# Hybrid attention block on one core: order of the opening products, and one gating weight's subtraction moved to VectorE

## The chip, the cores and the metric

The kernel runs on one core of a Trainium2 chip. A core has a TensorE (PE, matrix products; PEld in the profile is its loading of weights), a VectorE (DVE), a ScalarE (ACT), a GpSimd (POOL) and a SyncE (SP), which here issues the DMA transfers. Each engine works through its own instruction queue in order and waits on semaphores for the others. The metric is the device time of one execution in microseconds (us): 604.07 for the kernel before, the median of three runs (603.5 to 606.83).

## The reference

One decoder layer on 512 tokens and 16 leading meta tokens, width 1024, in float32:

```
u    = RMSNorm(h)                      # h: meta tokens, then x
proj = u @ w_in                        # 7600 columns, split into the parts below
(cq, ckv, k_pe, z_mla, fq, fk, fv, f, z_fox, gate_a, gate_b) = split(proj)
q, k, v of MLA   from RMSNorm(cq) @ w_uq and RMSNorm(ckv) @ w_ukv, with rope on 32 dims
o_mla = causal_attention(q, k, v);      y_mla = (o_mla * silu(z_mla)) @ w_br_mla
o_fox = causal_attention(fq, fk, fv, + cumulative log forget gate from f)
y_fox = (o_fox * silu(z_fox)) @ w_br_fox
mixed = (sigmoid(gate_a) * y_mla + sigmoid(gate_b) * y_fox) @ w_out
h + RMSNorm(mixed), meta tokens dropped
```

Both branches have 16 heads.

## The kernel before

Every float32 operand of a product is split into an upper half (rounded to the format that TensorE takes) and a lower half (the rest), and each product is three products: upper by upper, lower by upper, upper by lower. The upper half of a weight (`wh`) is a cast on ScalarE (line 130), its lower half (`wl`) a subtraction, `split_lo` (line 103), on the engine that `low[0]` holds: GpSimd until the merge at the end, VectorE there. A unit of work (`unit`) has a `prep`, which does cast and subtraction of its weight, and a list of steps with TensorE's products; who calls `prep` early decides where the subtraction comes in the queues.

The opening turns five token tiles (0 to 3 with 128 tokens, 4 with the 16 meta tokens) into normalized, transposed features, `uTh` (upper, by ScalarE, line 382) and `uTl` (lower, by VectorE, line 379). Then `small` multiplies a tile's features by the narrow part of `w_in` (432 columns: latent query and key, rope key, forget gate). That weight comes in four chunks `wsr` of two row blocks each. Its upper half is `wsh`: chunks 0 to 2 are cast by GpSimd, chunk 3 by ScalarE after tile 1's features (`small_hi`, line 313). Its lower half is `wsl`: chunk 0 by GpSimd, chunks 1 to 3 by VectorE (`small_lo`, line 317). The products of tile t gather in the PSUM tile `psm` t; argument 2 of `small` says which of the three products are issued, argument 3 which of the eight row blocks. After them come `back` (the square sums at line 418, the rope pieces `tm` at line 423, which wait for the square sums, and the scalings) and `latent` (transposes).

The order on TensorE is the order in which the program is written (`manual_schedule`). The calls with `pin` also keep the written order on their engines; the other work on ScalarE, VectorE, GpSimd and SyncE is ordered by a scheduler that plans with estimated durations.

Then come 16 attention stages, FoX and MLA in turn for eight pairs of heads. A stage has the scores of its own pair (`st`), the softmax in two parts (`n0`, `n1`: exponentials, `ri`, the normalized weights `pn` as an upper half from ScalarE and a lower half from VectorE at line 823, and small pieces for the meta tokens, `mt`, on GpSimd), the transposes of `pn` into `pt` by DMA, and the product with the values (`ov`), which is issued in the next stage. Between them TensorE gets "fill": products that project the next pair (`mq`, `mk`, `fq`, `fk`, `v`) and the gating products (`z`). In the first stage (`si == 0`) the preparation of the next two weights of the fill, `mq`'s and that of the second gating product, is called between `n0()` and `n1()`. After the stages the merge multiplies by the branch weights and `w_out`.

Of the kernel before, what the change touches and what calls it, by code (L numbers as in the profile page):

```python
# [27 lines left out]
KD = D // 128  # L28
# [26 lines left out]
def block_kernel(ctx: ExitStack, tc: tile.TileContext, x, meta_tokens, pre_norm_g, w_in, fox_forget_b,  # L55
                 mla_q_norm_g, mla_kv_norm_g, w_uq, w_ukv, w_br_mla, w_br_fox, w_out, post_norm_g,
                 rope_tok, rope_pe, out):
    nc = tc.nc
# [37 lines left out]
    def mm(*a, **k):  # L96
        nc.tensor.matmul(*a, **k)  # L97
# [25 lines left out]
    low = [nc.gpsimd]  # L123
# [46 lines left out]
    def acc(name):  # L170
        return accp.tile([128, 512], F32, tag="acc", name=name)
# [49 lines left out]
    def run(steps):  # L221
        for _, fn in steps:
            fn()
# [48 lines left out]
    with ExitStack() as ph:  # L272
# [124 lines left out]
        def small(t, which, ks=range(KD)):  # L397

            d0, q0 = (META + 128 * t, 0) if t < 4 else (0, R_Q)
            if t not in psms:  # L400
                psms[t] = acc("psm4")[:, 0:NSM] if t == 4 else pps.tile([128, NSM], F32, tag="psm", name=f"psm{t}")
            ts = slice(d0, d0 + 128)
            for k in ks:
                for q, (u, w) in enumerate(((uTh, wsh), (uTl, wsh), (uTh, wsl))):
                    if q in which:
                        mm(psms[t][:, q0:], u[:, k, ts], w[:, k, q0:], start=(k == 0 and q == 0),
                           stop=(k == KD - 1 and q == 2))
# [68 lines left out]
        turned(1, 1, range(KD), pin)  # L476
        pin(small_hi(3, nc.scalar.copy))
        small(0, (1,), range(2))
        small(0, (0, 1), range(2, KD))
        small(1, (0, 1))  # L480
        for c in (1, 2, 3):
            pin(small_lo(c, nc.vector))
        squares(2, pin)
# [72 lines left out]
    with ExitStack() as att:  # L556
# [352 lines left out]
        for si, (br, pr) in enumerate(stages):  # L909
            s0, s1, n0, n1, va = attention(br, pr)  # L910

            fill = fills[si]
            for fn in [s0] + late:
                fn()
            if si == 0:
                run(fill[:3])
            s1()

            if si == 0:

                run(fill[3:5])
                run(vts[1, 0] + pe_rest)
                n0()
                for ahead_ in [fn.prep for _, fn in fill[5:] if hasattr(fn, "prep")][:2]:
                    ahead_()
                n1()
                first_t.extend(through)
                run(fill[5:])
            else:
                if si == 1:  # L930

                    written[0] = True
                    for x in range(2):
                        store0(x, 2, 8)
                    written[0] = False
                run(fill[:5])
                if si == 1:

                    behind[:] = exps[:1]
                if si == 2:  # L940
                    behind.clear()
                n0()
                run(fill[5:11])
                if br:

                    behind[:] = [halved[("k", 1, pr), 1]]
                run(fill[11:12])
                if br:
                    behind.clear()
                n1()  # L950
                if 6 <= si < 8:

                    written[0] = True
                    rest1(si - 6)
                    written[0] = False
                run(fill[12:])
            written[0] = False
            if si == 1:

                behind[:] = [halved[("k", 1, 1), 0]]  # L960
            late = [va]
# [232 lines left out]
```

## Time and profile before

| | |
|---|---|
| median of three runs | 604.07 us (603.5 to 606.83) |
| profiled execution | 606.64 us, of which the span is 604.9 us |
| PE busy | 592.8 us (98%) |
| DVE, ACT, POOL busy | 375.2, 342.9, 180.8 us (62%, 57%, 30%) |
| opening | until the first scores at 59.84 us |
| first attention stage | 59.84 to 81.31 us |
| moved by DMA | 93.25 MB |

The span is the time from the first to the last instruction of the profiled execution; its own time is 1.74 us longer. A busy share is a sum over the instructions of an engine. An entry such as "PE z <- POOL wl" in the list of waits says that TensorE stood idle before a product that writes `z` until GpSimd had finished `wl`; its numbers are the total, the count and the longest. Where a line of the timeline carries brackets, they hold the idle time before it and what ended it.

### The profile page before, as it was taken

To read this page: it belongs to the slowest core of one execution; us is meant where nothing else is said; L and a number is where in the kernel's file an instruction comes from. 1 tells how busy PE (TensorE), PEld (TensorE's weight loads), DVE (VectorE), ACT (ScalarE), POOL (GpSimd) and SP (SyncE) were. 2 spreads that over 40 slices of the span, in tenths; PEclk is the share of its full clock that TensorE was granted. 3 is DMA by queue.
4 is the path that set the end of the run, shared out by engine and by line. 5 is a ranking of instruction groups with operands and counts; after the bars stand their busy time and mean duration, and the time that the engine had idled before them with its cause. 6 is when DMAs were issued, how large, how long until landed. Compare 5 with 4: busy or idle time off the path is not lost.

```text
span 604.9 us, 11000 instructions
## 1 busy us (share of the span) xinstructions
PE 592.8 (98%) x3777; PEld 503.7 (83%) x3777; DVE 375.2 (62%) x1003; ACT 342.9 (57%) x786; POOL 180.8 (30%) x240
## 2 busy tenths in 40 slices
PE   8999999999999999999999999999999999999996
PEld 6989789889889888788898898887888888888884
DVE  6846776774775775755756657773833624367857
ACT  7846775784674775755766748761221433243653
POOL 4316644444348453523433534530000000000000
PEclk9999999999999999989999999999999999999999
DMA  8533589789796898988797885987633323322603
GB/s 295 113 79 106 123 198 215 182 198 205 108 191 163 162 180 186 165 194 165 132 177 170 168 184 136 198 169 258 194 105 104 101 77 101 104 98 91 232 0 140
DMA packets 219960, 93.25 MB, mean 154 GB/s; under 512 B 133420, under 2 KB 211636, under 8 KB 219904
## 3 DMA queue, kind: packets, MB, share of 16 engines
q1 hardware_dynamic: 219904, 92.55, 66.3%
q8 instruction: 30, 0.49, 0.3%
q14 instruction: 26, 0.21, 0.1%
HBM read 58.10 MB, written 4.00 MB: 103 GB/s over the span
## 4 chain that ended last, share of the span: by engine, by line
PE 95%; DVE 2%; ACT 1%; POOL 1%; DMA 1%; issue 0%; DVEq 0%; POOLq 0%; ACTq 0%
PE z L97 15%; PE py L97 14%; PE pg L97 14%; PE v L97 9%; PE st L97 8%; PE fk L97 8%; PE fq L97 7%; PE ov L97 5%; PE x L97 4%; PE psm L97 3%; PE mq L97 2%; PE mk L97 1%; PE ppe L97 1%; PE spun L97 1%; PE y L97 1%; PE pt L100 1%
## 5 line engine op out<-in xcount | busy, mean ns | idle before, releaser
L103 POOL TENSOR_TENSOR wl<-wraw,wh 128x1024 fp32r<-128x1024 f32 (+2 forms) x63 | 122.6, 1954 | 106.2 <-ACT wh L130 74.4
L130 ACT CAST wh<-wraw 128x1024 fp32r<-128x1024 f32 (+1 forms) x80 | 83.1, 1041 | 116.7 <-PE pg L97 38.5
L823 DVE SCALAR_TENSOR_TENSOR pn<-sf,ri,pn 128x128 f16<-128x128 f32 (+3 forms) x128 | 70.8, 593 | 13.8 <-ACT pn L822 13.7
L795 ACT ACTIVATE sf<-sf,nb 128x144 f32<-128x144 f32 (+3 forms) x128 | 72.0, 564 | 11.1 <-DVE nb L787 10.9
L822 ACT ACTIVATE pn<-sf,ri 128x128 f16<-128x128 f32 (+3 forms) x128 | 61.5, 551 | 20.1 <-ACT sf L795 17.3
L103 DVE TENSOR_TENSOR wl<-wraw,wh 128x1024 fp32r<-128x1024 f32 x33 | 40.3, 1222 | 41.2 <-ACT wh L130 41.1
L787 DVE CUSTOM_DVE_ANT_0 sf<-st,maskt 128x272 f32<-128x272 f32 (+2 forms) x128 | 48.7, 435 | 4.2 <-PE st L97 4.1
L97 PE MATMUL z<-uTh,wl 128*128 128x512 f32 x128 | 50.1, 391 | 1.1 <-POOL wl L103 1.1
L97 PE MATMUL z<-uTh,wh 128*128 128x512 f32 x128 | 50.9, 398 | 0.0
L97 PE MATMUL pg<-uTh,wh 128*128 128x512 f32 x128 | 50.3, 393 | 0.0
L97 PE MATMUL z<-uTl,wh 128*128 128x512 f32 x128 | 50.0, 391 | 0.0
L97 PE MATMUL pg<-uTl,wh 128*128 128x512 f32 x128 | 49.8, 389 | 0.0
L97 PE MATMUL pg<-uTh,wl 128*128 128x512 f32 x128 | 49.8, 389 | 0.0
L97 PE MATMUL py<-gh,wh 128*128 128x512 f32 x128 | 49.8, 389 | 0.0
L97 PE MATMUL py<-gl,wh 128*128 128x512 f32 x128 | 49.8, 389 | 0.0
L97 PE MATMUL py<-gh,wl 128*128 128x512 f32 x128 | 49.8, 389 | 0.0
L97 PE MATMUL st<-hlk,hlq 64*128 64x272 f32 (+3 forms) x480 | 48.0, 310 | 0.0
L97 PEld LDWEIGHTS st<-hlk,hlq 64*128 64x128 f32 x480 | 35.7, 189 | 5.9 <-ACT vh L719 2.8
L700 DVE TENSOR_REDUCE vsc<-v 128x1 f32<-128x272 f32 (+1 forms) x32 | 13.2, 432 | 37.9 <-PE v L97 37.9
L97 PE MATMUL v<-uTh,wl 128*128 128x256 f32 (+1 forms) x128 | 36.5, 285 | 0.0
L97 PE MATMUL fk<-uTl,wh 128*128 128x256 f32 (+1 forms) x128 | 36.5, 285 | 0.0
L97 PE MATMUL fk<-uTh,wh 128*128 128x256 f32 (+1 forms) x128 | 36.4, 285 | 0.0
(233 smaller groups left out, 1432.4 us busy)
## 6 DMA issues: line engine op xcount, KB each, us to landing
wraw<-in_w_in_dram SPq DMA_DIRECT2D x56, 512.0 KB, 4.4
wraw<-in_w_br_fox_dram SPq DMA_DIRECT2D x8, 512.0 KB, 3.5
tb<-in_w_out_dram SPq DMA_DIRECT2D x8, 512.0 KB, 8.2
wraw<-in_w_br_mla_dram SPq DMA_DIRECT2D x8, 512.0 KB, 3.5
wraw<-in_w_out_dram SPq DMA_DIRECT2D x6, 512.0 KB
pt<-pn SPq DMA_TRANSPOSE x128, 3.2
xr<-in_x_dram SPq DMA_DIRECT2D x4, 512.0 KB, 6.0
out_dram<-yo SPq DMA_DIRECT2D x8, 256.0 KB, 2.0
```

The lines of the kernel that those rows point to most:

```text
L97: nc.tensor.matmul(*a, **k)
L100: nc.tensor.transpose(*a)
L103: return eng.tensor_tensor(out=lo, in0=src, in1=f32(hi), op=ALU.subtract)
L130: nc.scalar.copy(wh[:, :n], raw[:, :n])
L700: nc.vector.tensor_reduce(out=sc[:, i : i + 1], in_=ps, op=ALU.max, axis=AX.X, apply_absolute_value=True)
L787: nc.vector.tensor_tensor_reduce(out=sf_of(h, b)[:, c0 : c0 + w], in0=ps[h][:, o : o + w], in1=maskt[:, m0 : m0 + w], scale=-scale, scalar ...
L795: exps[g] = nc.scalar.activation(sf, sf, AF.Exp, bias=sums["nb"][:, h, b : b + 1], scale=-1.0, accum_out=sums["su"][:, h, b : b + 1]).ins
L822: nc.scalar.activation(hi, sf, AF.Copy, scale=rib)
L823: nc.vector.scalar_tensor_tensor(out=lo, in0=sf, scalar=rib, in1=hi, op0=ALU.mult, op1=ALU.subtract)
```

## The change

Two edits. In the opening, the products of the features' upper and lower halves with `wsh` (products 0 and 1) were issued for all of tile 0 and then for all of tile 1; now both tiles' row blocks up to 5, which use chunks 0 to 2, come first, and the row blocks 6 and 7 of both tiles, which use chunk 3, after them. In the first attention stage, `low[0]` is VectorE while the two preparations between `n0()` and `n1()` are called. `mq`'s preparation names GpSimd itself and is not touched; the second gating weight's lower half is now subtracted on VectorE.

```diff
         small(0, (1,), range(2))
-        small(0, (0, 1), range(2, KD))
-        small(1, (0, 1))
+        small(0, (0, 1), range(2, 6))
+        small(1, (0, 1), range(6))
+        small(0, (0, 1), range(6, KD))
+        small(1, (0, 1), range(6, KD))
         for c in (1, 2, 3):
             pin(small_lo(c, nc.vector))
...
                 n0()
+                low[0] = nc.vector
                 for ahead_ in [fn.prep for _, fn in fill[5:] if hasattr(fn, "prep")][:2]:
                     ahead_()
+                low[0] = nc.gpsimd
                 n1()
```

On TensorE 12 products of tile 1 (`psm1`) now stand ahead of the last four of tile 0 (`psm0`); the number of products is the same. The scheduler also orders ScalarE differently in the opening. In the piece below, of ScalarE's queue, `psm` is tile 0's, `hn_301` is the normalization of token tile 3, `sm_315` and `st_0_316` take tile 0's square sums, and line 332 is the square root behind each sum.

```order
 L332 ACTIVATE st_4_296<-st_4_296,eps_t 16x1
+L418 ACTIVATE sm_315,st_0_316<-psm_216 128x256
 L352 ACTIVATE hn_301,st_3_302<-ht_148 128x1024
-L418 ACTIVATE sm_315,st_0_316<-psm_216 128x256
+L418 ACTIVATE sm_315,st_0_316<-psm_216 128x128
 L332 ACTIVATE st_3_302<-st_3_302,eps_t 128x1
-L418 ACTIVATE sm_315,st_0_316<-psm_216 128x128
-L382 ACTIVATE uTh<-pt_0_330,gcol 128x128
 L332 ACTIVATE st_0_316<-st_0_316,eps_t 128x2
```

Tile 3's square sum stands now between the two square sums of tile 0's features, where it stood ahead of both, and its square root moves back with it. On VectorE the scaling of `hn_301` moves back in the same way, to stand between the `tm` pieces.

In the first attention stage VectorE's queue held, before, after the second part's `ri_872`: the two lower halves `pn_725`, the finishing of the first gate `sil_1049`, the lower halves of the next query and key.

```order
L803 TENSOR_SCALAR su_871<-su_871 128x2
L804 RECIPROCAL ri_872<-su_871 128x2
L823 SCALAR_TENSOR_TENSOR pn_725<-sf_923,ri_872,pn_725 128x4x128 x2
L736 SCALAR_TENSOR_TENSOR sil_1049<-sil_1049,z_961 128x512
L103 TENSOR_TENSOR hlq_1061<-mq_1054,hlq_1061 128x512
L103 TENSOR_TENSOR hlk_1080<-mk_1076,hlk_1080 128x272
```

The same place of VectorE's queue now (`wl_1012` is the second gating weight's lower half):

```order
L805 TENSOR_SCALAR su_871<-su_871 128x2
L806 RECIPROCAL ri_872<-su_871 128x2
L103 TENSOR_TENSOR wl_1012<-wraw_855,wh_1011 128x1024
L825 SCALAR_TENSOR_TENSOR pn_725<-sf_923,ri_872,pn_725 128x4x128
L738 SCALAR_TENSOR_TENSOR sil_1049<-sil_1049,z_961 128x512
L825 SCALAR_TENSOR_TENSOR pn_725<-sf_923,ri_872,pn_725 128x4x128
L103 TENSOR_TENSOR hlq_1061<-mq_1054,hlq_1061 128x512
L103 TENSOR_TENSOR hlk_1080<-mk_1076,hlk_1080 128x272
```

The subtraction stands ahead of both `pn_725`, and `sil_1049` has come between them. On GpSimd `wl_1012` is gone from its place behind the small pieces of `pn_725`. On SyncE a load of a later weight no longer waits for GpSimd, and in the next stage the transpose of `vh` into `vp` goes ahead of a load of `CT`. From the third stage on the queues are the same.

## The prediction

> **What bounds the kernel now.** I read the page first (busy shares), then the waits of TensorE over the whole span, then the timeline of each engine round the places where TensorE waits.
>
> ```profile
> span 604.9 us, 11000 instructions
> PE 592.8 (98%) x3777; PEld 503.7 (83%) x3777; DVE 375.2 (62%) x1003; ACT 342.9 (57%) x786; POOL 180.8 (30%) x240
> ...
> PE spun L97 <- DVE ONE L236: 2.1, 1, 2.1
> PE ov L97 <- issue: 1.2, 1, 1.2
> PE ov L97 <- DMA pt<-pn: 1.2, 1, 1.2
> PE z L97 <- POOL wl L103: 1.1, 1, 1.1
> PE psm L97 <- ACT wsh L313: 0.6, 1, 0.6
> ```
>
> TensorE is busy 98% of the span, and the list of its waits is short: 2.1 us at the very start, 2.4 us before one product of attention weights and values (`ov`), 1.1 us before a gating product (`z`) and 0.6 us before a feature product of the opening (`psm`). The change speaks to the last two. No other engine can give more than what such waits hold, since TensorE keeps its instruction count.
>
> The time is worked out against the profiled execution, 606.64 us (span 604.9 and 1.74 around it). That is 2.57 us above the median of 604.07, nearly the 2.4 us of the `ov` wait. I take it that the ordinary run lacks most of that wait; one profile cannot prove it. Differences found in this execution are put on the median.
>
> **Part 1, the opening.** In these timeline rows the columns are start, duration, engine, line and operation.
>
> ```profile
> 11.80 0.36 PE L97 MATMUL psm<-wsh,uTh 128*128 128x432 f32 x1
> 12.00 0.36 PE L97 MATMUL psm<-wsh,uTl 128*128 128x432 f32 x1
> 13.01 0.46 PE L97 MATMUL psm<-wsh,uTh 128*128 128x432 f32 x1 [0.65 <-ACT wsh L313]
> ...
> 7.79 4.36 ACT L382 ACTIVATE uTh<-pt,gcol 128x128 fp32r<-128x128 f32 x16
> 11.99 0.96 ACT L313 CAST wsh<-wsr 128x864 fp32r<-128x864 f32 x1
> ...
> 9.15 4.21 DVE L379 SCALAR_TENSOR_TENSOR uTl<-pt,gcol,uTh 128x128 fp32r<-128x128 f32 x16
> 13.29 2.98 DVE L317 TENSOR_TENSOR wsl<-wsr,wsh 128x864 fp32r<-128x864 f32 x3
> ```
>
> These products follow each other every 0.20 us (11.80 to 12.00). After the one at 12.00 the next could start at 12.20; it started at 13.01, since it reads the fourth chunk's upper half, which ScalarE finished at 11.99 + 0.96 = 12.95. So the hole costs 13.01 - 12.20 = 0.81 us.
>
> The change puts 12 products of token tile 1 there, 12 x 0.20 = 2.4 us, from 12.20 to 14.6, when the fourth chunk has been ready for 1.6 us. They need tile 1's features. Their upper halves are the last eight of ScalarE's 16, done by 12.15. Their lower halves are the last eight of VectorE's 16 at 4.21 / 16 = 0.263 us: chunk 0 at 9.15 + 9 x 0.263 = 11.52 (needed at 12.40), chunk 5 at 12.83 (needed at 14.4). The cover is full, so 0.81 us comes forward. The work queued behind (VectorE's three lower halves of the small weights, 13.29 to 16.27) waits for the fourth chunk, not for TensorE, and does not move; the last is due at 14.6 + 8 x 0.20 + 6 x 0.20 = 17.4.
>
> What is late next is tile 4's lower features. The scheduler now puts the square sum of `hn3` on ScalarE behind the first square sum of the features, and VectorE's pieces follow.
>
> ```profile
> 17.17 1.06 ACT L352 ACTIVATE hn<-ht 128x1024 f32<-128x1024 f32 x1 [1.29 <-DVE hn L358]
> 18.83 0.38 ACT L418 ACTIVATE sm<-psm 128x256 f32<-128x256 f32 x1 [0.51 <-PE psm L97]
> 19.54 0.20 ACT L418 ACTIVATION_READ_ACCUMULATOR sm<-psm 128x1 f32 x1
> ...
> 20.44 0.75 DVE L358 TENSOR_SCALAR hn<-ht,st 128x1024 f32<-128x1024 f32 x1
> 21.10 0.41 DVE L423 TENSOR_TENSOR tm<-psm,rt 128x16 f32<-128x16 f32 x4
> 21.50 0.21 DVE L103 TENSOR_TENSOR uTl<-um,uTh 128x64 fp32r<-128x64 f32 x1
> ...
> 21.88 0.24 PE L97 MATMUL psm<-wsh,uTh 128*128 128x176 f32 x1
> 21.96 0.28 PE L97 MATMUL psm<-wsh,uTl 128*128 128x176 f32 x1
> ...
> 24.96 1.04 PE L100 MATMUL pt<-ident,hn 128*128 128x128 f32 x8
> ```
>
> Tile 0's features end 0.81 earlier, so the first square sum starts at 18.02, not 18.83. Then `hn3` takes ScalarE for about 1.06 us, the second square sum reads out by about 19.8, and VectorE's `tm` pieces, which wait for it, start there. The `hn3` scaling (its neighbours show 0.66 us from its start to the next start) falls between them, so the lower half `uTl<-um` comes at 19.8 + 0.2 (two `tm`) + 0.2 (reciprocal) + 0.66 + 0.2 (last `tm`, reciprocal) = 21.05 and ends at 21.26. TensorE, 0.81 us earlier, wants it for the product of 21.96 at 21.05 with its load before. So about 0.2 us is given back; bounds are 0 (the old order would have it at 20.9) and the whole 0.81. I take 0.2, which the rows of these very instructions give. **Part 1: 0.81 - 0.2 = 0.6 us.** Later pieces of the opening (transposes of tile 3 need `hn3`, which is done at about 21.0 and was used at 24.96) move forward with TensorE, which by the list of its waits has none from there to the `z` product of part 2.
>
> **Part 2, the first attention stage.**
>
> ```profile
> 72.83 0.40 PE L97 MATMUL z<-uTh,wh 128*128 128x512 f32 x1
> 73.07 0.39 PE L97 MATMUL z<-uTl,wh 128*128 128x512 f32 x1
> 74.57 0.50 PE L97 MATMUL z<-uTh,wl 128*128 128x512 f32 x1 [1.11 <-POOL wl L103]
> 76.67 0.28 PE L97 MATMUL mk<-cTh,wh 128*128 128x256 f32 x1
> ...
> 69.83 1.04 ACT L130 CAST wh<-wraw 128x1024 fp32r<-128x1024 f32 x1
> ...
> 70.81 0.24 POOL L809 TENSOR_TENSOR mt<-sf,ri 128x32 f32<-128x32 f32 x1 [3.97 <-DVE ri L804]
> 71.64 2.88 POOL L103 TENSOR_TENSOR wl<-wraw,wh 128x1024 fp32r<-128x1024 f32 x1
> ...
> 71.53 3.53 DVE L823 SCALAR_TENSOR_TENSOR pn<-sf,ri,pn 128x512 f16<-128x512 f32 x2 [1.22 <-ACT pn L822]
> 75.58 0.68 DVE L103 TENSOR_TENSOR hlq<-mq,hlq 128x512 fp32r<-128x512 f32 x1
> ...
> L103 DVE TENSOR_TENSOR wl<-wraw,wh 128x1024 fp32r<-128x1024 f32 x33 | 40.3, 1222 | 41.2 <-ACT wh L130 41.1
> ```
>
> The upper half of this weight is ready at 69.83 + 1.04 = 70.87. GpSimd first does four small pieces (70.81 to 71.64), then the subtraction for 2.88 us, to 74.52. TensorE would have started the product at 73.07 + 0.24 = 73.31 (the spacing of 72.83 and 73.07) and started at 74.57: 1.26 us lost. VectorE is idle for 1.22 us before 71.53, takes 1.22 us for such a subtraction (the group row), and can have it done at 70.87 + 1.22 = 72.1. If it first sat through all four pieces of GpSimd it would end at 71.67 + 1.22 = 72.9, still before 73.31. So the wait goes: **1.26 us**, both bounds giving the same.
>
> What now stands behind it on VectorE: the two `pn` pieces of the softmax, `sil`, `hlq`. Behind `hlq` waits TensorE's `mk` (a PSUM buffer), at 76.67 - 1.26 = 75.41. The price of a `pn` piece decides.
>
> ```profile
> 244.79 1.42 DVE L823 SCALAR_TENSOR_TENSOR pn<-sf,ri,pn 128x512 f16<-128x512 f32 x2 [0.84 <-ACT pn L822]
> ...
> 77.03 1.37 SPq L91 DMA_TRANSPOSE pt<-pn  x1
> pt<-pn SPq DMA_TRANSPOSE x128, 3.2
> ...
> 83.60 2.04 PE L97 MATMUL ov<-pt,vp 80*64 80x512 f16 x26
> ```
>
> The same two pieces took 1.42 us in a later stage, with GpSimd at rest, and 3.53 us here, beside its subtraction. That subtraction is gone, so I take 0.71 each: 72.1 + 0.71 + 0.68 + 0.71 + 0.68 = 74.9, 0.5 us ahead of `mk`.
>
> [...]
>
> The transposes of `pn` are issued on SyncE back to back, the last at 77.03, so an earlier `pn` moves them little. With the page's median of 3.2 us to land they are there at 80.2, and `ov` now comes at 83.60 - 1.26 = 82.3: covered by 2.1 us. SyncE's one exchange (the `vp` transpose ahead of a `CT` load) and the weight load that no longer waits for GpSimd have no waiter on TensorE; I cost them at nothing.
>
> **Sum:** 0.6 + 1.26 = 1.86 us. From the median: 604.07 - 1.86 = 602.2 us (profiled execution: 606.64 - 1.86 = 604.8). That is 0.3%, inside the 0.5% (3.0 us) which is about what a measurement of this kernel can tell from no change.
>
> **Rivals.** *Late transposes.* The other wait is in a stage that the change does not touch.
>
> ```profile
> 254.44 3.48 DMA pt<-pn
> ...
> 256.48 0.38 PE L97 MATMUL ov<-pt,vp 80*64 80x512 f16 x1 [1.20 <-issue]
> ...
> SPq L91 <- DMA qpe_dram<-gT: 4.7, 1, 4.7
> ```
>
> There `ov` was ready at 256.48 - 1.20 = 255.28, and the last transposes landed at 254.44 + 3.48 = 257.92, since SyncE stood 4.7 us for a store. It decides on whether the landing is before 255.28. If the shifted kernel does this in its usual run, the 2.57 comes back: 602.2 + 2.57 = 604.8, slower than before by 0.7 us; in two stages 607.3. For it: one of the three runs was 606.83, like the profile. Against: the order of all queues is the same from the third stage on, and every load there is released by TensorE's own progress.
>
> *Transposes better.* If the usual run still carries part of that wait (604.07 against the lowest, 603.5, hints at some) and the shift removes it, up to 2.35 goes: 599.9 to 602.2, middle 601.0.
>
> *Opening swallowed.* The order of `hn3` costs all of 0.81 instead of 0.2: 604.07 - 1.26 = 602.8. For it: VectorE's rows of that place follow each other without a gap, so any slip is passed on. Against: the sum above.
>
> *Stretched VectorE.* With `pn` at 3.53 / 2 = 1.77, `hlq` ends at 72.1 + 2 x 1.77 + 2 x 0.68 = 77.0, 1.6 us after `mk` wants it, and part 2 becomes a loss of 1.6 - 1.26 = 0.3: 604.07 - 0.6 + 0.3 = 603.8. Against: what stretched it is removed.
>
> **Chances.** Forecast (602.2, own range 601.4 to 602.8) 0.54; late transposes 0.15, a third of that with two stages; transposes better 0.15; opening swallowed 0.11; stretched 0.05. The range 600.9 to 604.9 leaves out the lower half of "better" (0.08), the double late case (0.05) and some scatter (0.05). Faster than 601.05 is most of "better": 0.13. Slower than 607.1 is the double late case and 0.01 of scatter: 0.06. The rest is 0.81.
>
> **What would show it.** Right: no TensorE wait for `wsh` nor for `wl` on GpSimd; the `wl` subtraction on VectorE at about 1.2 us, ending some 1 us before its product; the two `pn` pieces at about 0.7 us each; TensorE's rows from 25 to 73 us about 0.6 us earlier than now, and those after 75 us about 1.9 us earlier. Wrong: a new wait of TensorE at tile 4's product beyond 0.3 us, at `mk` for `hlq`, or at any `ov` for transposes; the last is the one that could undo the sum, for it is larger than both gains.

## The result, and the profile after

The changed kernel takes 606.63 us (median of 22 runs, 603.03 to 609.56) against 604.07 us for the kernel before (22 runs beside it, 602.81 to 606.83): ratio 1.0038, 95% interval 1.0022 to 1.0054. It is slower by 0.4%, about 2.6 us, where 602.2 us had been forecast. The profiled execution took 605.73 us, its span 603.9 us.

Both edits did what they say. The list of TensorE's waits after the change (engine and operation that waits, what it waits for: total us, times, longest) holds neither `z <- POOL wl` nor `psm <- ACT wsh` any more, but new ones:

```profile
PE spun L97 <- DVE ONE L236: 2.1, 1, 2.1
PE ov L97 <- DMA pt<-pn: 2.0, 2, 1.4
PE ov L97 <- PE st L97: 0.9, 1, 0.9
PE pc L100 <- ACT uTh L382: 0.4, 1, 0.4
PE psm L97 <- POOL wsh L313: 0.3, 1, 0.3
```

The first stage, in the timeline after the change (start us, duration us, engine, line, operation; in brackets the idle time before and what ended it): the subtraction on VectorE, the pieces of `pn`, `sil` and `hlq` behind it, and TensorE's product with `wl`.

```profile
71.79 1.24 DVE L103 TENSOR_TENSOR wl<-wraw,wh 128x1024 fp32r<-128x1024 f32 x1 [0.58 <-ACT wh L130]
72.96 0.74 DVE L825 SCALAR_TENSOR_TENSOR pn<-sf,ri,pn 128x512 f16<-128x512 f32 x1
...
74.88 0.68 DVE L103 TENSOR_TENSOR hlq<-mq,hlq 128x512 fp32r<-128x512 f32 x1
...
73.97 0.39 PE L97 MATMUL z<-uTl,wh 128*128 128x512 f32 x1
74.20 0.39 PE L97 MATMUL z<-uTh,wl 128*128 128x512 f32 x1
```

The subtraction takes 1.24 us and ends at 73.03, 1.2 us before its product at 74.20, which follows its neighbour without a gap. A `pn` piece takes 0.74 us, `hlq` is there at 75.56. All of this is as forecast.

The opening, after the change: TensorE at the first of tile 4's products and at the transposes of tile 1 (`pc`), then two rows of VectorE between them; and the same rows of the kernel before (second fence).

```profile
22.05 0.24 PE L97 MATMUL psm<-wsh,uTh 128*128 128x176 f32 x1
...
29.12 0.63 PE L100 MATMUL pc<-ident,sm 128*128 128x128 f32 x4 [0.35 <-ACT uTh L382]
...
25.67 1.99 DVE L425 TENSOR_TENSOR sm<-tm 128x32 f32<-128x32 f32 x1
...
28.70 0.27 DVE L103 TENSOR_TENSOR KPL<-pc,KPH 32x128 fp32r<-32x128 f32 x1
```

```profile
21.88 0.24 PE L97 MATMUL psm<-wsh,uTh 128*128 128x176 f32 x1
...
28.22 0.62 PE L100 MATMUL pc<-ident,sm 128*128 128x128 f32 x4
...
25.11 1.65 DVE L425 TENSOR_TENSOR sm<-tm 128x32 f32<-128x32 f32 x1
...
27.80 0.27 DVE L103 TENSOR_TENSOR KPL<-pc,KPH 32x128 fp32r<-32x128 f32 x1
```

In this execution the first weight chunk was ready later: TensorE's first products with `uTl` came 0.79 us later than in the profile before (10.93 against 10.14). The first of tile 4's products is only 0.17 us later, so 0.62 us had been won; the second waits for its lower half, and 0.40 is left behind it (the third starts at 22.46, before at 22.07). At `pc` TensorE is 0.90 us later than before: the gain is gone by 30 us. The list of waits names ScalarE's `uTh` there, which these transposes don't read. Of what they do need, the last to end is VectorE's `KPL`, which reads tile 0's `pc` out of the only buffer of that name: it ends at 28.97, 0.15 us ahead of them, and in the kernel before at 28.07, again 0.15 us ahead of them (28.22). So there was no slack at `pc` before the change either. VectorE comes to `KPL` behind tile 1's row `sm<-tm`.

The second stage's product with the values, the place where the rest went. After the change, SyncE's last two transposes of that stage and TensorE's `ov`; below them the same rows of the kernel before:

```profile
102.24 3.44 SPq L91 DMA_TRANSPOSE pt<-pn  x2
...
106.75 0.38 PE L97 MATMUL ov<-pt,vp 80*64 80x512 f16 x1 [0.93 <-PE st L97]
107.72 2.01 PE L97 MATMUL ov<-pt,vp 80*64 80x512 f16 x25 [0.59 <-DMA pt<-pn]
```

```profile
100.53 3.61 SPq L91 DMA_TRANSPOSE pt<-pn  x2
...
106.22 2.04 PE L97 MATMUL ov<-pt,vp 80*64 80x512 f16 x26
```

After the change SyncE has issued the transposes at 105.68, and the main part of `ov` starts 2.04 us behind that. Apply the same 2.04 us to the kernel before: 104.14 + 2.04 = 106.18, and `ov` started at 106.22 without a wait. TensorE had next to no slack there, about 0.1 us. Whatever it wins ahead of 106 us is worth nothing unless the transposes come earlier too.

### The profile page after: what moved, and what is told of

Its sections match the earlier page's. It is cut to its first block, busy times and chain, and to the rows that moved or that the text cites. A ratio compares the mean times of both kernels' runs of the same rounds, so it can differ in the third digit from the quotient of the medians.

```text
span 603.9 us, 10999 instructions
## 1 busy us (share of the span) xinstructions
PE 592.4 (98%) x3777; PEld 503.0 (83%) x3777; DVE 374.5 (62%) x1004; ACT 342.9 (57%) x786; POOL 180.1 (30%) x239
## 4 chain that ended last, share of the span: by engine, by line
PE 94%; DMA 2%; ACT 2%; DVE 1%; issue 0%; SPq 0%; POOL 0%; DVEq 0%; ACTq 0%; POOLq 0%
PE z L97 16%; PE pg L97 15%; PE py L97 14%; PE v L97 9%; PE st L97 8%; PE fk L97 8%; PE fq L97 7%; PE ov L97 5%; PE x L97 4%; PE psm L97 3%; PE mq L97 2%; DMA pt<-pn 1%; PE mk L97 1%; PE ppe L97 1%; PE y L97 1%; DMA wsr<-in_w_in_dram 1%
## 5 line engine op out<-in xcount | busy, mean ns | idle before, releaser
L103 POOL TENSOR_TENSOR wl<-wraw,wh 128x1024 fp32r<-128x1024 f32 (+2 forms) x62 | 119.8, 1940 | 107.6 <-ACT wh L130 78.5
L825 DVE SCALAR_TENSOR_TENSOR pn<-sf,ri,pn 128x128 f16<-128x128 f32 (+3 forms) x128 | 68.8, 576 | 12.5 <-ACT pn L824 12.5
L103 DVE TENSOR_TENSOR wl<-wraw,wh 128x1024 fp32r<-128x1024 f32 x34 | 41.6, 1222 | 42.5 <-ACT wh L130 42.3
L97 PE MATMUL ov<-pt,vp 128*64 128x256 f16 (+4 forms) x416 | 33.7, 307 | 3.0 <-DMA pt<-pn 2.0
```

The lines of the kernel that those rows point to most:

```text
L103: return eng.tensor_tensor(out=lo, in0=src, in1=f32(hi), op=ALU.subtract)
L825: nc.vector.scalar_tensor_tensor(out=lo, in0=sf, scalar=rib, in1=hi, op0=ALU.mult, op1=ALU.subtract)
```

## The experiments

Three theories. S (slack): the time goes at the second stage's `ov`, where TensorE stands for transposes. C (clock): the same, and a long stand is followed by a lower granted clock. (A stand is idle time of TensorE.) Q (queue): SyncE's changed order alone. In the first set they have the letters E (S without the clock), Q, and O (the opening's order). Spare products, where a kernel has them, write a PSUM tile that nobody reads; they are work on top, and nothing of the layer is left out in any kernel.

**The opening's edit alone.**

```diff
-        small(0, (0, 1), range(2, KD))
-        small(1, (0, 1))
+        small(0, (0, 1), range(2, 6))
+        small(1, (0, 1), range(6))
+        small(0, (0, 1), range(6, KD))
+        small(1, (0, 1), range(6, KD))
```

> Opening edit alone (both tiles' row blocks 0 to 5 first), first stage as before. Theory E (TensorE comes early to the products with the values and finds the transposes late, because SyncE and the DMA queue keep their own pace from the first stage on): the opening shifts everything together, so it gains what is left of the 0.8 us hole, 603.3 to 604.1. Theory Q (the changed order of SyncE's queue in the second stage makes the transposes late): SyncE's order is as before here, so the same 603.3 to 604.1. Theory O (the scheduler's new order in the opening costs the time): 606 or more.

Measured: 604.41 us (12 runs), ratio 1.0011, interval 0.9999 to 1.0024; just above what E and Q expected. Here the opening starts as in the profile before (10.13 against 10.14), so the rows can be compared as they stand. The first and third of tile 4's products and `pc`:

```profile
21.05 0.24 PE L97 MATMUL psm<-wsh,uTh 128*128 128x176 f32 x1
...
21.45 0.27 PE L97 MATMUL psm<-wsl,uTh 128*128 128x176 f32 x1
...
28.10 0.63 PE L100 MATMUL pc<-ident,sm 128*128 128x128 f32 x4 [0.35 <-ACT uTh L382]
```

Before, they stood at 21.88, 22.07 and 28.22. So 0.83 us is won at the first, 0.62 at the third, behind the wait for its neighbour's lower half, and 0.12 at `pc`. TensorE reaches the first stage's `ov` at 83.45, before at 83.60: 0.15 us of the 0.62 arrive. The row `sm<-tm` starts 0.46 us earlier on VectorE (24.65) but takes 1.99 us (1.65 before) and ends only 0.12 earlier, beside GpSimd's subtraction of a weight, which follows ScalarE (three of them from 24.32 to 30.32 us in the profile before, where the row starts at 25.11). And ScalarE's square sum of tile 1 starts at 22.39, before at 22.53: `hn3`, which it did before while it waited for tile 0's products (17.17), now stands behind them (18.37). This is read from the rows; no run puts `hn3` back.

**The first stage's edit alone.**

```diff
+                low[0] = nc.vector
                 for ahead_ in [fn.prep for _, fn in fill[5:] if hasattr(fn, "prep")][:2]:
                     ahead_()
+                low[0] = nc.gpsimd
```

> First-stage edit alone (the gating weight's lower half on VectorE), opening as before. Theories E and Q: about 606 to 607, most of the loss seen with both edits, and a wait of TensorE at the second stage's product with the values (about 106 us) that was not there before. Theory O: the 1.26 us wait goes and stays gone, 602.8.

Measured: 604.74 us (9 runs), ratio 1.0018, interval 1.0007 to 1.0029. The first stage's `ov` starts at 82.32, 1.28 us earlier than before, as forecast, and the second stage's then stands 2.6 us. Its timeline there, and the stretches behind it (from and to us, length, busy us and count of PE, PEld, DVE, ACT, POOL, then the granted clock, DMA share, GB/s):

```profile
107.01 0.38 PE L97 MATMUL ov<-pt,vp 80*64 80x512 f16 x1 [2.00 <-issue]
107.98 2.68 PE L97 MATMUL ov<-pt,vp 80*64 80x512 f16 x25 [0.59 <-DMA pt<-pn]
...
108.00:110.00 2.00, 2.00 (x22) 1.66 (x22) 0.09 (x1) 1.88 (x8) 1.27 (x1) 0.79 1.11 326
110.00:112.00 2.00, 2.00 (x20) 1.79 (x18) 1.38 (x4) 1.61 (x5) 1.15 (x4) 0.50 1.20 252
112.00:114.00 2.00, 2.00 (x14) 1.57 (x12) 1.99 (x10) 1.31 (x3) 0.00 (x0) 0.86 1.17 306
```

So more than the gain is lost at one place: 1.28 won, 2.6 stood, and then a stretch at half clock. Read as time at 0.50, the three rows are 0.84 + 2.00 + 0.56 = 3.4 us (for the first, (1 - 0.79) x 2 / 0.5), which costs 1.7 us. The time lies between what E and Q (606 to 607) and O (602.8) expected; the wait came as E and Q had it.

**The stage's edit with spare products in place of the removed wait** (1.27 us of them, behind the first fill steps; the planner then puts both `CT` loads ahead of the `vp` transpose).

```diff
-                run(fill[5:])
+                run(fill[5:14])
+                spare = ovp.tile([128, 512], F32, tag="ov", name="spare")
+                for w in (512, 512, 512, 512, 512, 256):
+                    mm(spare[:, :w], ONE, uTh[:, 0, META : META + w], start=True, stop=True)
+                run(fill[14:])
```

> First-stage edit alone, and 1.27 us of spare products on TensorE just where the removed wait stood (five of 512 columns, one of 256, into a PSUM tile nobody reads), so that TensorE goes on as late as before; SyncE's order falls back nearly to that of before (the transpose of vh goes behind both CT loads). Theory E: back to the time of before, 603.6 to 604.6. Theory Q: also near it. If the subtraction on VectorE itself costs time: 606 or more.

Measured: 604.50 us (11 runs), ratio 1.0010, interval 0.9997 to 1.0023; 0.86 us of stand at the second stage's `ov`, clock 0.999 over the span. With 1.27 us more work it is no slower than the edit alone (604.74). By itself this is within the noise; the later sets repeat it with a larger gap.

**The kernel before with only SyncE's new order** (`vp` transpose, `CT`, weight load, `CT`).

```diff
-                    with tc.issue_after(first_t[0]) if pr == 1 else nullcontext():
+                    with tc.issue_after(turned_v[0, 0]) if pr == 1 else nullcontext():
```

> The kernel before with SyncE's changed order alone (in the second stage the transpose of vh ahead of both loads of CT, the second of them behind a weight load), everything else as before. Theory Q: 606 or more, with the wait at the second stage's product with the values. Theory E: 604.1, within 0.4 of before.

Measured: 604.69 us (12 runs), ratio 1.0015, interval 0.9996 to 1.0035. The order alone may cost some tenths; it isn't the 2.6 us.

**The changed kernel once more, for a profile of a longer execution.**

> The changed kernel itself, unaltered, beside the others of this set. Three theories of the lost 2.6 us. S (slack): TensorE reaches the second stage's `ov` earlier than the transposes of `pn` can land, and stands 1.5 to 2.6 us there, so nothing won before that place is kept. C (clock): S, and a stand of more than about 2 us is followed by a lower granted clock, which costs another 1.5 us and makes the usual run slower than the profiled one. Q (queue): the loss is SyncE's changed order alone, whatever TensorE does. All expect 606.0 to 607.0. C expects, in a profile above 606 us, a stretch of 20 us or more with a granted clock under 0.96 behind the `ov` of the second or a later stage; S alone expects a clock of 1.00 there and longer waits in its place.

Measured: 607.31 us (12 runs, 603.68 to 611.16), ratio 1.0045, interval 1.0017 to 1.0074. The profiled execution took 608.10 us:

```profile
103.66 3.88 SPq L91 DMA_TRANSPOSE pt<-pn  x2
...
108.62 0.60 PE L97 MATMUL ov<-pt,vp 80*64 80x512 f16 x1 [2.87 <-issue]
109.60 3.79 PE L97 MATMUL ov<-pt,vp 80*64 80x512 f16 x25 [0.38 <-DMA pt<-pn]
...
106.00:108.00 2.00, 0.00 (x0) 0.00 (x0) 1.40 (x8) 0.61 (x1) 0.00 (x0) 0.88 1.25 265
108.00:110.00 2.00, 1.00 (x4) 0.46 (x6) 0.00 (x0) 2.00 (x8) 1.48 (x1) 0.50 1.11 222
110.00:112.00 2.00, 2.00 (x14) 1.29 (x12) 0.36 (x2) 1.49 (x7) 0.87 (x1) 0.50 1.14 336
112.00:114.00 2.00, 2.00 (x21) 1.79 (x19) 0.57 (x1) 2.00 (x6) 1.15 (x4) 0.50 1.21 294
114.00:116.00 2.00, 2.00 (x19) 1.69 (x18) 1.75 (x8) 0.49 (x1) 0.00 (x0) 0.91 0.86 232
```

The stand is 3.25 us, and the clock is at 0.50 for 0.48 + 6.00 + 0.36 = 6.8 us. The 25 products that took 2.01 us above take 3.79 here. C had expected this fall behind a longer stand; S alone had not.

Every execution in the experiments, profiled or not, and every one of the changed kernel has its mean granted clock on record. No profile without a stretch at half clock behind its first 4 us shows less than 0.997. (The figure is coarse: one with 3.4 us at half clock still shows 0.997.) Of the 34 executions of the changed kernel (22 of the result, 12 here), 22 are under 0.997; they took 606.20 to 611.16 us, median 607.68. The other 12 took 603.03 to 606.36 us, median 604.42. Of the 106 executions of the kernel before that ran beside the experiments, 8 are under 0.997 (median 607.97), and the median of the other 98 is 604.10. So by this figure the clock falls in about two executions of three of the changed kernel and in one of thirteen of the kernel before. Where it does not, 0.3 us is left of the difference: nearly all of the 2.6 us comes with the fall, as the stand and the half clock together. The stage's edit alone has 2 such executions of 9, the opening's alone none of 12.

**The changed kernel with spare products in the stand itself** (eight, planned as 1.7 us, 2.12 us busy in its profile, between the third stage's scores and the second stage's `ov`; the planner also moves some `pn` pieces of the third stage ahead of `gT`).

```diff
-            for fn in [s0] + late:
+            s0()
+            if si == 2:
+                spare = ovp.tile([128, 512], F32, tag="ov", name="spare")
+                for _ in range(8):
+                    mm(spare, ONE, uTh[:, 0, META : META + 512], start=True, stop=True)
+            for fn in late:
```

> The changed kernel with eight spare products of 512 columns (about 1.7 us of TensorE work into an unused PSUM tile) between the third stage's first scores and the second stage's `ov`, that is, in the place where TensorE stands. The planner also moves one or two `pn` pieces of the third stage ahead of `gT` on VectorE, and two small loads of `CT` behind transposes. C: TensorE no longer idles 2 us, the clock stays at 1.00, and the time falls by about 1.5 us to 604.6 to 605.4, with more work than before. S without C: the products only take the place of the wait, 606.4 to 606.9. If the wait were no part of the loss, the products would cost their 1.7 us: 608.3.

Measured: 606.00 us (10 runs, 605.08 to 607.31), 1.3 us less than the unaltered changed kernel beside it (607.31), with about 2 us more work; ratio to before 1.0026, interval 1.0005 to 1.0047. In its profile TensorE stands 0.20 us at the second stage's `ov` and the clock stays at 1.00 from 84 to 130 us; 1.6 us of stand come at 257 us. None of the 10 executions has a mean clock under 0.997, where 9 of the 12 beside it have one. The median lies between what C and S expected, and the two intervals overlap. A fall of the clock that no longer comes explains how more work can be faster; what the planner moved on VectorE is not separated from it here.

**The changed kernel with a `CT` load ahead of the `vp` transpose again.**

```diff
-                    with tc.issue_after(first_t[0]) if pr == 1 else nullcontext():
+                    with tc.issue_after(first_t[0]) if pr == 1 else nullcontext(), \
+                            tc.high_priority(offset=180) if pr == 1 and h == 0 else nullcontext():
```

> The changed kernel with a `CT` load planned ahead of the `vp` transpose again on SyncE, as it stood before the change (the weight load stays ahead of the second `CT` load). No other engine's order changes. Q: most of the loss goes, 604.3 to 604.9. S and C: the transposes start at most 0.4 us earlier, the wait stays over 1 us, 605.8 to 606.7.

Measured: 606.92 us (6 runs), ratio 1.0054, interval 1.0034 to 1.0074; 3.6 us of stand, then 3.4 us at half clock. Q falls.

**The changed kernel with two thirds of the rope queries' stores moved behind the second stage's transposes.**

```diff
-                        store0(x, 2, 8)
+                        store0(x, 2, 4)
...
+                if si == 2:
+                    with tc.issue_after(through[0]):
+                        for x in range(2):
+                            store0(x, 4, 8)
```

> The changed kernel with the four stores of the rope queries cut in two: two heads of each (all that the next pair needs) where the stores stood, the other four heads only after the second stage's transposes. This takes 0.5 MB of transfers out from in front of those transposes. S and C: SyncE reaches the transposes 1.5 to 2.5 us earlier, the wait at the second stage's `ov` falls below 0.5 us, the clock stays, and the gains are kept: 602.0 to 603.5, less if the later stores hold up the third stage's transposes. Q: no change, 606.0 to 607.0.

Measured: 610.15 us (6 runs), ratio 1.0101, interval 1.0074 to 1.0128. A miss for S and C as I had put them: SyncE had issued the transposes only at 107.17, hardly earlier than in the 608.10 us profile (107.54) and later than in the first one (105.68), and the later stores led to more stands (four at an `ov`, 3.4 us in all, beside one of 2.9). The clock is at half for 3.4 us twice, behind 109 us and behind 263 us.

**The kernel before, for a second profile.**

> The kernel before, unaltered, for a second profile of it. S and C: SyncE's last transposes of the second stage end between 104 and 106 us as in the profile shown, TensorE is at that `ov` at about 106.2 and stands less than 1 us there, the clock stays at 1.00 in that place. Rival: SyncE is as late in the kernel before as in the changed one (over 107 us), and the slack told nothing. Time 603.5 to 605.5.

Measured: 604.02 us, span 602.2 us.

```profile
102.50 3.58 SPq L91 DMA_TRANSPOSE pt<-pn  x2
...
107.30 0.40 PE L97 MATMUL ov<-pt,vp 80*64 80x512 f16 x1
108.13 2.01 PE L97 MATMUL ov<-pt,vp 80*64 80x512 f16 x25 [0.43 <-DMA pt<-pn]
```

Issue ends at 106.08, and 2.05 us later the main part runs, with 0.43 us of stand. The opening of this execution ran 1.07 us later (products with `uTl` from 11.21), so all is shifted; the lack of slack is the same as in the first profile.

**The changed kernel with spare products where `wl` was waited for** (nine, planned as 1.9 us, 2.1 us in its profile).

```diff
-                run(fill[5:])
+                run(fill[5:14])
+                spare = ovp.tile([128, 512], F32, tag="ov", name="spare")
+                for w in 9 * (512,):
+                    mm(spare[:, :w], ONE, uTh[:, 0, META : META + w], start=True, stop=True)
+                run(fill[14:])
```

> The changed kernel with nine spare products of 512 columns (about 1.9 us of TensorE work into an unused PSUM tile) where TensorE waited for GpSimd's `wl` before the change, so that TensorE reaches the second stage's `ov` when it did before, though all that the change freed on the other engines stays. The planner puts both `CT` loads ahead of the `vp` transpose on SyncE. S and C: with more work it is faster than the changed kernel by 2 us: 604.0 to 605.2, the wait at the second stage's `ov` under 1.2 us, clock 1.00. If the loss came from SyncE or from the other engines' changed timing and not from TensorE's early arrival, the spare work comes on top: 607.5 to 609.

Measured: 605.23 us (12 runs, 604.02 to 606.73), ratio 1.0015, interval 1.0002 to 1.0028, against 1.0038 and 1.0045 for the changed kernel without the extra work. From 60 us on, its list of waits has one entry, and that is at 257 us:

```profile
PE ov L97 <- issue: 1.3, 1, 1.3
```

Holding TensorE back removes the stand at 106 us, and none of the 12 executions has a mean clock under 0.997. So it is TensorE's early arrival that makes the stand, not what the change does on VectorE and GpSimd. SyncE's order moves too here (both `CT` loads ahead of the `vp` transpose), but with one of them moved alone TensorE stood 3.6 us. It did not run side by side with the changed kernel, and the intervals of the ratios overlap (up to 1.0028 here, from 1.0022 and 1.0017 there); the profile is the clearer evidence.

**The changed kernel with those stores on GpSimd's queue.**

```diff
-                    dma(qpe_dram[8 * g + a : 8 * g + b, i, x], results(x)[16 * a : 16 * b, i])
+                    dma(qpe_dram[8 * g + a : 8 * g + b, i, x], results(x)[16 * a : 16 * b, i],
+                        None if g else nc.gpsimd.dma_start)
```

> The changed kernel with the four stores of the rope queries issued on GpSimd's DMA queue in place of SyncE's; SyncE's order behind them is then CT, CT, vp, weight load. S and C, if SyncE's own issuing is what holds the transposes: SyncE is 3 to 4 us earlier from 82 us on, as the four stores took 3.2 to 4.6 us of its time, the wait at the second stage's `ov` goes, 602.0 to 603.2, which would beat both kernels. If the DMA engines' pace holds them (their share in 84 to 108 us was 0.89 to 0.97): no gain, 605.5 to 607.5, since the same bytes move. GpSimd's issue time may also delay its next `wl`, which would show as a TensorE wait for `wl`.

Measured: 605.41 us (12 runs), ratio 1.0023, interval 1.0005 to 1.0041. SyncE is free of the stores, yet its `vp` transpose then takes 6.00 us of its time (4.36 in the changed kernel), the transposes are issued at 106.95, and GpSimd's `wl` is late once (0.7 us). The stretch from 84 to 108 us in the profiles of the kernel before (second profile), the one with moved stores and this one, in that order (columns as above):

```profile
84.00:108.00 24.00, 23.70 (x201) 20.98 (x198) 17.06 (x55) 16.22 (x41) 14.22 (x16) 1.00 0.99 199
```

```profile
84.00:108.00 24.00, 21.30 (x179) 19.64 (x174) 15.99 (x47) 13.32 (x31) 11.40 (x15) 1.00 0.94 166
```

```profile
84.00:108.00 24.00, 22.23 (x184) 19.98 (x180) 16.34 (x44) 14.03 (x32) 11.89 (x16) 1.00 1.08 201
```

The DMA engines' share is 0.94 to 1.08 in all three, with 166 to 201 GB/s. Neither fewer bytes in front nor less issuing on SyncE brought the transposes forward (issued by 107.17 and 106.95 us, in the changed kernel by 105.68 and 107.54); what sets their pace isn't shown.

**Moving `ov` instead of filling the stand.** First the second stage's `ov` behind four fill steps of the third stage, then the ninth stage's too, then both moves in the kernel before. No work is added.

```diff
-            for fn in [s0] + late:
+            s0()
+            m = {2: 4, 9: 3}.get(si, 0)
+            run(fill[:m])
+            for fn in late:
...
-                run(fill[:5])
+                run(fill[m:5])
```

The first of the three has `{2: 4}` there.

> The changed kernel with the second stage's `ov` issued behind the first fill steps of the third stage (the `vp` transpose and three row blocks of the gating product, about 2.1 us of work that TensorE does later otherwise). No work is added. S and C: the stand at that place shrinks below 0.8 us, the clock stays at 1.00, and the 1.3 to 1.9 us that TensorE had won by then are kept up to the `ov` at 257 us, where the known wait can take back 1 to 2 us of it: 602.5 to 604.5. If what costs the time is not this stand, the move changes nothing: 606 to 607.5.

Measured: 605.71 us (12 runs, 603.38 to 610.32), ratio 1.0021, interval 1.0001 to 1.0041. The stand at the second stage's `ov` is 0.6 us in its profile, as S and C expected; the time is not, since 2.0 us of stand at the third stage's `mk` and 1.8 us at the ninth stage's `ov` came in its place, each followed by 3.4 us at half clock (610.32 us in that execution).

> As the last, and also the ninth stage's `ov` (at 257 us) behind three fill steps of the tenth. S and C: both stands gone, 601.5 to 603.2, faster than both kernels. If moving `ov` back holds up the next stage's transposes or scores instead, a new wait of TensorE for `st` or for transposes shows in the next stage, 603 to 605.

Measured: 605.58 us (12 runs), ratio 1.0009, interval 0.9995 to 1.0023. A miss: no version of this set beats both kernels.

> The kernel before with the same two moves of `ov`, without the change. Together with the last it says what the change itself is worth once neither `ov` waits. S and C: before loses only its wait at 257 us (0 to 2.35 us) and 0.4 us at the second stage, 602.8 to 603.8; the difference to the last is then the predicted gain of the change, 1.3 to 1.9 us. If the change is worth nothing by itself, both are equal.

Measured: 605.13 us (12 runs, one of them of 1269.39 us, which the ratio leaves out), ratio 1.0010, interval 0.9993 to 1.0027. A miss too: 602.8 to 603.8 had been expected, and a gain of the change over it. The change is worth nothing here either: with both `ov` moved, the two kernels are equal within their intervals. The waits from 60 us on show why. The changed kernel with both moves, and a stretch of its clock:

```profile
PE mk L97 <- DVE sil L738: 1.4, 1, 1.4
PE mk L97 <- DVE hlq L103: 0.6, 1, 0.6
...
120.00:122.00 2.00, 1.45 (x7) 1.15 (x6) 1.09 (x2) 0.62 (x3) 2.00 (x1) 0.73 0.61 117
122.00:124.00 2.00, 2.00 (x6) 1.59 (x5) 0.42 (x1) 0.20 (x1) 0.04 (x1) 0.50 1.07 204
124.00:126.00 2.00, 2.00 (x12) 1.75 (x12) 1.10 (x4) 0.90 (x1) 0.00 (x0) 0.91 1.00 208
```

and the kernel before with both:

```profile
PE z L97 <- POOL wl L103: 1.1, 1, 1.1
PE mk L97 <- DVE hlq L103: 0.6, 1, 0.6
PE mk L97 <- DVE sil L736: 0.4, 1, 0.4
```

The stand at 106 us is gone in both. The early TensorE stands 13 us later, at 119 us, for VectorE (2.0 us against 1.0), and again the clock is at 0.50 for 3.4 us. It looks as if the softmax and its transposes as a whole were as long as TensorE's work in the second and third stage, and not one transfer late; no run here shortens them, so this is an argument and not shown.

## Why the prediction was wrong, step by step

- **Part 2, the first stage: right, size too.** The wait of 1.26 us went, the subtraction took 1.24 us (forecast 1.22), `pn` 0.74 a piece (0.71), `hlq` was early enough. With this edit alone the first stage's `ov` came 1.28 us earlier. The stretched-VectorE rival did not come. GpSimd's small pieces took longer beside VectorE's new subtraction and the `pn` piece behind it (two casts of 0.21 us each before, now 1.09 from 72.02 us and 0.72 from 73.05), without a waiter.
- **Part 1, the opening: right up to tile 4, then wrong.** With the opening's edit alone, 0.83 us was won at the first of tile 4's products (the sum had 0.81) and 0.62 behind the wait for the lower half (0.6). But the sum ended at that place, with the words that TensorE has no wait from there on. `pc`, 7 us later, had no slack, and the chain on ScalarE and VectorE ahead of it moved by 0.12 us. 0.15 us reached the first stage. The rival "opening swallowed" had the right outcome at another place; its reason, the order of `hn3`, fits ScalarE's rows.
- **The cover of `ov` was worked out for the first stage alone, and what SyncE does behind it was put at nothing ("have no waiter on TensorE; I cost them at nothing"): the step that failed.** The cover in the first stage was enough (no wait there in any profile). The next `ov`, 22.6 us later, had about 0.1 us, which the timeline of before could have told: the end of SyncE's last transposes plus the 2.05 us that they need, against the start of `ov`. The exchange on SyncE was not what cost the time (the order alone gave no such loss), but its transposes are what TensorE waits for next. The gain taken at 1.86 us was therefore 0 at that place, whatever its two parts were.
- **Late transposes was the right rival, at the wrong place and too cheap.** I put it at 255 us, where a wait was on show, and gave it 2.57 us and 0.15. It came at 106 us, in both profiles of the changed kernel, at 1.5 and 3.3 us, and it has a second half that the sum did not contain: the clock. In the 608.10 us profile, TensorE reaches the first `ov` 1.97 us earlier than in the second profile of before (82.71 against 84.68) and the third one 3.70 us later (131.29 against 127.59). Those 5.67 us are 2.82 of stand (3.25 - 0.43), and some 2.7 for the half clock (6.8 us, of which 1.5 were stood through anyway: 5.3 x 0.5); 0.2 is not accounted for.
- **"Wrong: ... at any `ov` for transposes; the last is the one that could undo the sum"** came true; late transposes had been given 0.15.
- **The wait at 257 us** does not explain the result. It is 2.35 us in one profile of before and absent in the other, 1.42 us in one of the changed kernel and absent in the other. But the prediction misread its price. It set 2.57 us, the distance of the profiled execution from the median, against 2.4 us of wait. The same profile shows the clock behind that wait (columns as above):

```profile
258.00:260.00 2.00, 2.00 (x22) 1.65 (x23) 0.36 (x2) 1.49 (x5) 1.15 (x4) 0.80 1.10 340
260.00:262.00 2.00, 2.00 (x20) 1.79 (x18) 1.27 (x3) 1.01 (x2) 0.00 (x0) 0.50 1.21 294
262.00:264.00 2.00, 2.00 (x17) 1.69 (x16) 1.73 (x8) 0.00 (x0) 0.00 (x0) 0.85 0.78 202
```

That is 0.80 + 2.00 + 0.60 = 3.4 us at half clock, so the wait cost 2.35 + 1.7 = 4.05 us there. The second profile of before bears it out: it is 2.62 us shorter although its opening ran 1.07 us later and it stood 0.43 us at 106 us, 4.1 us in all. The price of a stand with the clock behind it was on show in the profile before.

What stays open: why the stand differs between executions of the same kernel (the two profiles of the changed kernel took 605.73 us with no fall of the clock and 608.10 us with 6.8 us at half clock). Nor is it settled why SyncE is later when TensorE is earlier: in the seven profiles in which the first `ov` starts by 82.9 us the second stage's transposes were issued at 105.7 to 107.5 us (mean 106.5), in the seven in which it starts after 83.4 at 104.1 to 106.1 (mean 105.4); the two between lie at 105.68 and 106.95. Whether weight loads that are released earlier do it, no run here separates.

## What to carry to other kernels

Before a gain on the bounding engine is counted, follow it stage by stage to the next place where that engine takes something from a transfer queue, and work out the slack there (end of issue, plus landing, against the start of the consumer): the gain is worth at most that slack as long as the transfers don't come earlier too, and here it was 0.1 us. A wait that is removed early can come back as a longer one (with the stage's edit alone 1.28 us were won and 2.6 us stood), and a stand costs more than itself when the clock falls behind it (those 2.6 us were followed by 3.4 us at a granted clock of 0.50, 1.7 us more); spare work that holds the engine back is a cheap test of both. The mean granted clock of the executions without a profile tells how often that happens. To make this kernel faster, the next thing to try, untested here, is to shorten the softmax and its transposes in the second and third stage.

## What the runs showed of the hardware

The granted clock fell at stands that come to 1.75 us or more. A single stand of 1.34 us left it at 1.00, as did 0.93 + 0.59 us and 0.68 + 0.93 us; 0.58 + 1.17 us, 1.40 + 0.56 us, 2.00 + 0.59 us and 2.87 + 0.38 us, each within some 3 us, were followed by a granted clock of 0.50 for 3.4, 3.4, 3.4 and 6.8 us. So it is in all 16 profiles: the nine pairs of stands at an `ov` or `mk` that come to 1.75 us or more are followed by half clock, and none that comes to 1.61 us or less is. What makes the clock fall, and what sets the length of the stretch, isn't shown. With the stage's edit alone the half clock began at 109.2 us, 1.2 us after the main part of `ov` had started; in the 608.10 us profile it began at 107.5 us, still in the stand.

Between the end of issue of the second stage's last two transposes and the main part of `ov` that waits for them lay 2.04 to 2.06 us in all four profiles above in which TensorE stood there (the changed kernel's two, the stage's edit alone, the second profile of before). And taking 0.5 MB out of the queue ahead of them, or issuing it elsewhere, did not bring them forward: their issue ended at 107.17 and 106.95 us, against 105.68 and 107.54 in the changed kernel.
